# Hybrid mixer: the block inverse and its transpose from vector-engine transpositions, the last doubling in three interleaved steps, the values' factor as a scale on the scalar engine

## The chip, the cores and the metric

The kernel runs on one core of a Trainium2 chip. The metric is the device time of one execution in microseconds; the median of several executions stands for a kernel. Five engines work side by side: the matrix engine (PE), the vector engine (DVE), the scalar engine (ACT), GpSimd (POOL) and the sync engine (SP), which issues the DMA transfers. Matrix products land in PSUM banks; DVE and ACT read them out into SBUF.

## What is computed

A two-layer network on 256 tokens of width 1024, in fp32: each layer is a feed-forward block, a mixer and another feed-forward block, each with a residual and a layer norm. The mixer of layer 0 is a hybrid of a gated delta rule and a state-space scan; that of layer 1 is sparse attention. The change lies in the delta rule of the hybrid mixer. Cut to what matters:

```python
def gated_delta_rule(q, k, v, g, beta):
    ...
    decay = decay_matrix(g_cum)
    strict = np.tril(np.ones((c, c), dtype=bool), -1)
    k_beta = k * beta[..., None]
    a_low = jnp.where(strict, jnp.einsum('bhncd,bhnsd->bhncs', k_beta, k) * decay, 0.0)
    rhs = jnp.concatenate([v * beta[..., None], k_beta * jnp.exp(g_cum)[..., None]], axis=-1)
    sol = lax.linalg.triangular_solve(a_low, rhs, left_side=True, lower=True, unit_diagonal=True)
    u, w = sol[..., :dv], sol[..., dv:]
    ...
    def step(state, inp):
        ...
        v_new = u_c - jnp.einsum('bhck,bhkv->bhcv', w_c, state)
        o_c = jnp.einsum('bhck,bhkv->bhcv', q_c, state) + jnp.einsum('bhcs,bhsv->bhcv', a_c, v_new)
        ...
```

There are 8 heads. k is normalised to length 1 first. The reference solves a unit lower triangular system per head and chunk; the kernel forms the inverse of the triangular matrix and multiplies with it.

## The kernel before

The kernel doesn't issue its instructions in the order in which they are written. All operations of the program are first collected by `Plan.add`; `Plan.order` (line 317) then simulates the engines with a price for every operation, and puts out one order for each engine; `Plan.emit` (line 497) issues it. That is why every instruction of the profile carries line 512: what tells groups apart are the tile names. At each step the planner takes, over all engines, the operation that can start earliest, and among those of one engine the one with the lower priority number (its place in the written program):

```python
key = (st if st > f + 1e-9 else f, p)
```

Here `f` is the time at which the engine is free, `st` the earliest start and `p` the priority. On PE, products that use only a quarter of the array (at most 64 rows of contraction) are told apart from the others; once such a product has run, every other product has 1,000,000 (`turn_pen`) added to `p`, so that quarters that are ready go on first. Operations written with `self.copy` may be put on ACT or DVE, whichever is free earlier. The planner also hands out the buffers: SBUF tiles of tag `m4` (36), weight landing tiles `raw` (4), PSUM banks `ps` (2), `mp` (2) and `acc` (4).

`hybrid` (line 1066) is woven from five strands by `weave` (line 745): `delta` (the delta rule), `space` (the convolutions of the values and of the scan's inputs), `gate`, `space2` (the scan) and `out_a` (half of the output projection). Dense projections go through the `ps` banks: each weight tile arrives in `raw`, is split into `whi` (ACT or DVE) and `wlo` (DVE), and three products of fp32r parts make one fp32 product. The projection's result is copied out of `ps` by ACT (tile `cv`), three DVE steps make the convolution, and ACT applies the nonlinearity.

In `delta` the 256 tokens are two blocks (b = 0, 1) of 128, each with two chunks of 64. Per block and head `AT` holds the transposed triangular matrix. Its inverse is built from 16x16 blocks:

- The 16x16 diagonal blocks are gathered by 32-partition copies into `Z` (in tile `sw`), transposed by one DVE transposition of 32x32 blocks into `Zt`, and inverted by 15 elimination steps on DVE (tile `W` in `sw`), for all blocks at once. After step 8 (`ZERO_AT`) a gate (`late`) releases DMA fills that write zeros into `Ys` and `Tt`.
- Two masked copies of `W` go to `Z`, a DVE transposition makes `Zt`, and narrow copies put the blocks onto the diagonal of `Y` (one tile per block of tokens). PE transposes each `Y` by heads (16 transpositions through `acc` banks), and copies of 64 partitions put the result into `X`. `Y` and `X` are the inverse in both forms.
- Two doublings (`lev` 4 and 5) join 16 to 32 and 32 to 64. Each does 32 products of `AT` with half of `X` into `pT`, a masked copy into `Tt`, then 32 products each into `pY` and `pX` that correct `Y` and `X`. Consecutive products lie in alternating quarters of the array.
- The last doubling joins the two chunks of 64: eight products of `AT` with `X` for each block into `pT[b]` (contraction over rows 0 to 63, result in partitions 64 to 127), a copy into `Tt`, then eight products of `Tt` with `Y` for each block into `pY[b]` (rows 64 to 127, result in partitions 0 to 63), subtracted from `Y`. All of one kind come before the other.

The values: in `space`, after their convolution (`vT`), PE transposes them four heads at a time into an `mp` bank, and one DVE operation for four heads multiplies with `rkinv`, the length of k (one factor for each token and pair of heads), into `vt`. `vt` is what the inverse is multiplied with.

Of fp32 products each shows as two records in the profile, transpositions and fp32r products as one.

Of the kernel before, what the change touches and what calls it, by code (L numbers as in the profile page):

```python
# [12 lines left out]
AF = mybir.ActivationFunctionType  # L13
OP = mybir.AluOpType
# [4 lines left out]
P = 128  # L19
# [31 lines left out]
def H3(t, h):  # L51
    return t.rearrange("p (h t) -> p h t", h=h)
# [483 lines left out]
class K:  # L536
# [529 lines left out]
    def hybrid(self, x, then):  # L1066
        self.arena = None
        nc, i = self.nc, self.i
        V = nc.vector
# [12 lines left out]
        pt = self.bank("mp")  # L1082
# [26 lines left out]
        pt = self.bank("mp")  # L1109
# [42 lines left out]
        def gdn_conv(dests, banks=("ps", "ps")):  # L1152
            for n in range(0, len(dests), 2):
                w = self.unit_cols(w_in, dests[n][0] * P, 256)
                for e in range(2):
                    c, dst = dests[n + e]
                    ps = self.bank(banks[e])[:, :T]
                    yield from self.proj_steps(x, w[e], ps)
                    self.conv_tile(ps, cw, 0, 16, c, None, dst)
# [6 lines left out]
        for n, src in enumerate((kT, qT)):  # L1166
            sq = H3(self.m4(1024, "sq"), 4)
            nc.scalar.activation(sq, src, AF.Square)
            for h in range(4):
                o, c = n * 4 + h, h % 2  # L1170
                nc.tensor.matmul(pn[c * 32:(c + 1) * 32], one_of[:, 31 - o:63 - o], sq[:, h, :],
                                 start=n == 0 and h < 2, stop=n == 1 and h > 1, tile_position=(0, c * 32))
# [13 lines left out]
        rkinv = self.sm([P, 2, 4], "rkinv")  # L1186
# [13 lines left out]
        def delta():  # L1200

            for b in range(2):
# [11 lines left out]
                AT = H3(self.m4(1024, f"AT{b}"), 8)  # L1214
# [9 lines left out]
            QS = [slice(32 * Q, 32 * Q + 32) for Q in range(4)]  # L1224
            sw = [self.m4(1024, f"sw{n}") for n in range(2)]
            z5 = lambda t: t.rearrange("p (r a b h) -> p r a b h", r=16, a=2, b=2)
            a4 = lambda t: t.rearrange("p (r a c) -> p r a c", r=16, a=2)
            Z, Zt = sw[0][:, :512], sw[0][:, 512:]
# [20 lines left out]
            for e in range(2):  # L1249
                V.tensor_scalar(a4(Z)[:, :, e, :], W, hm[:, e:e + 1], None, OP.mult)  # L1250
            V.transpose(Zt, Z)

            X, Tt = (H3(self.m4(1024, n, "D"), 16) for n in ("X", "T"))
            Ys = [H3(self.m4(1024, f"Y{b}", "D"), 8) for b in range(2)]
            with late:
                for t in Ys + [Tt]:
                    self.zero(t)
            CP = [slice(0, 64), slice(64, 128)]
            for b, Y in enumerate(Ys):
                for Q in range(4):  # L1260
                    self.copy(Y[QS[Q], :, QS[Q]].rearrange("p h (a r) -> p h a r", a=2),
                              z5(Zt)[QS[Q], :, :, b, :].rearrange("p r a h -> p h a r"))
                for q in range(2):
                    yield
                    pt = self.bank("acc")
                    for h in range(4):
                        nc.tensor.transpose(pt[:, h * P:(h + 1) * P], Y[:, q * 4 + h, :], self.ident)
                    for cp in CP:
                        self.copy(X[cp, b * 8 + q * 4:b * 8 + q * 4 + 4, :], H3(pt, 4)[cp, :, cp])
                blk[b]['Y'] = Y  # L1270
            AT = [d['AT'] for d in blk]
            heads = [(b, h, cp, b * 8 + h) for b in range(2) for h in range(8) for cp in CP]
            for lev in (4, 5):
                n = 1 << lev
# [5 lines left out]
                pT = self.bank("acc")  # L1280
# [4 lines left out]
                pX, pY = self.bank("acc"), self.bank("acc")  # L1285
                for b, h, cp, k in heads:
                    nc.tensor.matmul(pY[cp, k * 32:(k + 1) * 32], Tt[cp, k, :], half(Ys[b][cp, :, cp], 1)[:, h],
                                     start=True, stop=True)
# [7 lines left out]
                if lev < 5:  # L1296
                    self.zero(Tt)

            yield
            pT = [self.bank("acc") for b in range(2)]  # L1300
            for b in range(2):
                for h in range(8):
                    nc.tensor.matmul(pT[b][64:128, h * 64:(h + 1) * 64], AT[b][0:64, h, 64:128], X[0:64, b * 8 + h, :],
                                     start=True, stop=True)
                self.copy(Tt[64:128, b * 8:b * 8 + 8], H3(pT[b], 8)[64:128])
            yield
            pY = [self.bank("acc") for b in range(2)]
            for b, Y in enumerate(Ys):
                for h in range(8):
                    nc.tensor.matmul(pY[b][0:64, h * 64:(h + 1) * 64], Tt[64:128, b * 8 + h, :], Y[64:128, h, 64:128],  # L1310
                                     start=True, stop=True)
                V.tensor_tensor(Y[0:64, :, 64:128], Y[0:64, :, 64:128], H3(pY[b], 8)[0:64], OP.subtract)

            kd = H3(self.m4(1024, "kd"), 8)
            pt = self.bank("acc")
# [9 lines left out]
            for b, d in enumerate(blk):  # L1325
# [3 lines left out]
                vt, Y, attnT = vts[b], d['Y'], d['attnT']  # L1329
# [29 lines left out]
            for b, d in enumerate(blk):  # L1359
                tb = slice(b * P, (b + 1) * P)  # L1360
                attnT, vn = d['attnT'], d['vn']
                o = H3(self.m4(1024, f"o{b}"), 8)
# [37 lines left out]
        def space():  # L1400
            nonlocal bcT, xT, snw
            vT = [H3(self.m4(1024, f"vT{n}"), 4) for n in range(2)]
            yield from gdn_conv([(8 + n, vT[n // 4][:, n % 4, :]) for n in range(8)])

            for b, d in enumerate(blk):
                tb = slice(b * P, (b + 1) * P)
                vt = H3(self.m4(1024, f"vt{b}"), 8)
                for q in range(2):
                    yield
                    pt = self.bank("mp")  # L1410
                    for h in range(4):
                        nc.tensor.transpose(pt[:, h * P:(h + 1) * P], vT[q][:, h, tb], self.ident)
                    V.tensor_tensor(vt[:, q * 4:q * 4 + 4, :].rearrange("p (h r) t -> p h r t", r=2),
                                    pt.rearrange("p (h r t) -> p h r t", h=2, r=2),
                                    rkinv[:, b, q * 2:q * 2 + 2, None, None].to_broadcast([P, 2, 2, P]), OP.mult)
                vts[b] = vt

            snw = self.m4(1024, "snw", "S")
            with self.late():
                nc.sync.dma_start(snw, i['ssd_norm_w'].partition_broadcast(P).rearrange("p a d -> p (a d)"))  # L1420
            bcT = H3(self.m4(1024, "bcT", "S"), 4)
            xT = [H3(self.m4(1024, f"xT{n}", "S"), 4) for n in range(2)]
            dests = [(8 + n, bcT[:, n, :]) for n in (0, 2, 1, 3)] + [(n, xT[n // 4][:, n % 4, :]) for n in range(8)]
            for n in range(0, 12, 2):
                ws = [self.unit_cols(w_in, 4112 + dests[n][0] * P, 256)] if n > 2 else []
                for e in range(2):
                    c, dst = dests[n + e]
                    w = ws[0][e] if ws else self.unit_cols(w_in, 4112 + c * P, P)[0]
                    ps = self.bank("ps")[:, :T]
                    yield from self.proj_steps(x, w, ps)  # L1430
                    self.conv_tile(ps, cw, 64, 12, c, cw[:, 112 + c:113 + c], dst)
                if n in (6, 10):
                    over.append(n)
# [72 lines left out]
        acc = []  # L1506

        def out_a():
# [3 lines left out]
            for s in range(4):  # L1512
                wo = self.unit_rows(w_out, 2 * s, 2, 0, D)
                for e in range(2):
                    for b in range(2):
                        for c in range(2):
                            cs = slice(c * 512, (c + 1) * 512)
                            self.mm3(acc[b][c], self.xb(oT[0], b, 2 * s + e), (wo[e][0][:, cs], wo[e][1][:, cs]),
                                     s + e == 0, False)
                        yield  # L1520
        self.weave(list(zip((delta(), space(), gate(), space2(), out_a()), W_HYB)))
        terms = []
        for s in range(4):
# [497 lines left out]
```

## Time and profile before

| | |
|---|---|
| median of 3 executions | 1125.7 us |
| lowest, highest | 1124.62, 1126.05 us |
| the profiled execution | 1125.37 us |
| its span | 1123.7 us |
| granted clock of PE | 0.998 |
| HBM read | 194.04 MB |

The span runs from the first to the last instruction; the rest of the execution's time lies around it. "Busy" of PE comes from matmul ends that are modelled, so neighbouring records overlap; where an exact cost is wanted, the distance from the start of one group to the start of the next is used. In rows of groups the columns are: engine, operation, tile written <- tiles read, shapes, count, then busy us and mean ns of one, then the idle time of the engine before them and what ended it. In the order of time they are: start us, length us, engine, operation, tiles, shapes, count, and in brackets the idle time before and its releaser. Small tiles share tiles called `arena`.

### The profile page before, as it was taken

The page shows a single profiled execution, that of the slowest core. Times are in us where ns is not written, and L with a number is a line of the kernel's source. Part 1 is how long each engine was busy: PE and PEld are TensorE (multiplying, and loading weights), DVE is VectorE, ACT ScalarE, POOL GpSimd, SP SyncE. Part 2 cuts the span into 40 slices and gives each one's busy share as a digit, 9 for nine tenths or more (in the row PEclk, how much of TensorE's full clock was granted, in tenths as well). Part 3 has the DMA queues.
Part 4 walks back from the last instruction along what each step waited for, and adds up shares of the span by engine and source line. Part 5 has one row for each costly group of instructions (what it writes and reads, how often), then busy time and mean ns, then how long its engine had stood idle before and what let it go on. Part 6 is the DMA issues. An engine that isn't in the chain of part 4 may idle for free.

```text
span 1123.7 us, 16474 instructions
## 1 busy us (share of the span) xinstructions
PE 1109.8 (99%) x6548; PEld 946.3 (84%) x6548; DVE 887.7 (79%) x1491; ACT 514.9 (46%) x916; POOL 60.5 (5%) x110
## 2 busy tenths in 40 slices
PE   9999999999999999999999999999999999999997
PEld 7888888899999888888888888888877768888886
DVE  6977768799979998777767967876879999777755
ACT  6635332277736565533433633432346656443320
POOL 1000000012001310000000000000002100000000
PEclk9999999999999999999999999999999999999999
DMA  9966562642833285755563756555435237755511
GB/s 332 326 227 199 186 213 80 187 132 61 247 130 114 76 263 187 262 188 188 187 216 121 250 200 192 188 190 154 150 95 206 76 120 241 239 188 192 183 38 37
DMA packets 148710, 198.37 MB, mean 177 GB/s; under 512 B 9341, under 2 KB 123418, under 8 KB 148634
## 3 DMA queue, kind: packets, MB, share of 16 engines
q1 hardware_dynamic: 148634, 197.33, 53.7%
q8 instruction: 51, 0.84, 0.3%
q14 instruction: 25, 0.20, 0.1%
HBM read 194.04 MB, written 1.05 MB: 174 GB/s over the span
## 4 chain that ended last, share of the span: by engine, by line
PE 88%; DVE 9%; ACT 1%; issue 1%; DMA 0%; DVEq 0%; POOL 0%; ACTq 0%; POOLq 0%
PE ps L512 50%; PE acc L512 32%; PE mp L512 5%; DVE wlo L512 2%; DVE cv L512 2%; DVE arena L512 1%; DVE sw L512 1%; DVE qs L512 1%; DMA raw<-in_nsa_w_out_dram 0%; DVE whi L512 0%; DVE AT L512 0%; ACT cv L512 0%; ACT L512 0%; DVE h L512 0%; DVE X L512 0%
## 5 line engine op out<-in xcount | busy, mean ns | idle before, releaser
L512 DVE TENSOR_TENSOR wlo<-raw,whi 128x1024 fp32r<-128x1024 f32 (+1 forms) x349 | 416.0, 1214 | 13.4 <-ACT whi L512 10.6
L512 PE MATMUL ps<-x,whi 128*128 128x512 f32 (+2 forms) x1584 | 369.8, 363 | 1.4 <-ACT cv L512 1.0
L512 PEld LDWEIGHTS ps<-x,whi 128*128 128x128 f32 (+1 forms) x1584 | 278.9, 188 | 45.9 <-ACT cv L512 2.3
L512 ACT ACTIVATE whi<-raw 128x1024 fp32r<-128x1024 f32 x263 | 265.0, 1051 | 15.2 <-DMA raw<-in_ffn_w_in_dram 7.4
L512 PE MATMUL acc<-whi,g 128*128 128x512 f32 x704 | 230.3, 391 | 0.0
L512 PE MATMUL ps<-x,wlo 128*128 128x256 f32 x1368 | 222.2, 283 | 0.0
L512 ACT ACTIVATE sg<-ps 128x256 f32<-128x256 f32 x156 | 60.0, 384 | 345.0 <-PE ps L512 345.0
L512 PEld LDWEIGHTS ps<-x,wlo 128*128 128x128 f32 x1368 | 197.6, 190 | 11.6 <-issue 0.4
L512 DVE TENSOR_TENSOR sg<-ps,sg 128x256 f32<-128x256 f32 (+1 forms) x158 | 67.4, 427 | 161.1 <-ACT sg L512 160.5
L512 PEld LDWEIGHTS acc<-whi,g 128*128 128x128 f32 x704 | 132.5, 188 | 26.0
L512 PE MATMUL acc<-wlo,g 128*128 128x512 f32 x352 | 138.1, 392 | 0.0
L512 PE MATMUL ps<-whi,x 128*128 128x512 f32 (+1 forms) x480 | 128.1, 385 | 0.0
L512 PEld LDWEIGHTS ps<-whi,x 128*128 128x128 f32 x480 | 86.1, 188 | 15.7 <-issue 0.9
L512 PEld LDWEIGHTS acc<-wlo,g 128*128 128x128 f32 x352 | 66.4, 189 | 10.9
L512 PE MATMUL acc<-whi,x 128*128 128x512 f32 x224 | 73.5, 403 | 1.6 <-DVE x L512 0.9
L512 PE MATMUL ps<-wlo,x 128*128 128x512 f32 (+1 forms) x240 | 67.0, 380 | 0.0
L512 DVE CAST whi<-raw 128x1024 fp32r<-128x1024 f32 (+1 forms) x86 | 59.1, 687 | 0.5 <-DMA raw<-in_nsa_w_out_dram 0.5
L512 POOL TENSOR_TENSOR lnve<-lnve,mhalf 128x1 f32<-128x1 f32 x12 | 11.5, 957 | 741.7 <-DVE lnve L512 741.7
L512 PEld LDWEIGHTS acc<-whi,x 128*128 128x128 f32 x224 | 41.1, 188 | 11.1 <-DVE x L512 1.7
L512 PEld LDWEIGHTS ps<-wlo,x 128*128 128x128 f32 x240 | 43.3, 188 | 7.8 <-issue 0.5
L512 ACT ACTIVATE sg<-sg 128x256 f32<-128x256 f32 x72 | 30.1, 418 | 34.8 <-DVE sg L512 34.7
L512 PE MATMUL acc<-wlo,x 128*128 128x512 f32 x112 | 43.2, 402 | 0.0
(258 smaller groups left out, 1011.0 us busy)
## 6 DMA issues: line engine op xcount, KB each, us to landing
raw<-in_ffn_w_in_dram SPq DMA_DIRECT2D x72, 1024.0 KB, 5.2
raw<-in_ffn_w_out_dram SPq DMA_DIRECT2D x44, 1024.0 KB, 5.0
raw<-in_hyb_w_in_dram SPq DMA_DIRECT2D x20, 1024.0 KB, 5.2
raw<-in_ffn_w_in_dram SPq DMA_DIRECT2D x32, 512.0 KB, 5.0
raw<-in_hyb_w_out_dram SPq DMA_DIRECT2D x8, 1024.0 KB, 5.2
raw<-in_nsa_w_in_dram SPq DMA_DIRECT2D x5, 1024.0 KB, 5.6
raw<-in_nsa_cmp_w_dram SPq DMA_DIRECT2D x4, 1024.0 KB, 5.9
raw<-in_nsa_w_out_dram SPq DMA_DIRECT2D x4, 1024.0 KB, 6.2
```

What stands on the lines that cost most here:

```text
L512: r = getattr(getattr(nc, eng), fn)(*[res(a) for a in args], **{k: res(a) for k, a in kw.items()})
```

## The change

Three edits in `hybrid`:

1. A second DVE transposition `Zx` of `Z`, read in another order, gives the blocks in the other form. `X` is filled from it by eight copies of 32 partitions, next to the eight of `Y`. The 16 transpositions on PE, their `acc` banks and the eight 64-partition copies are gone. As the new copies write only the diagonal blocks, `X` gets a zero fill by DMA, between those of `Ys` and `Tt`.
2. The last doubling is written in three steps: the first block's eight products into `pT`; then, one by one, the second block's into `pT` and the first block's into `pY`, which lie in opposite quarters; then the second block's into `pY`. Both subtractions come after.
3. The values' factor is applied by ACT, as the scale of a copy out of PSUM: two heads at a time (eight operations of 256 columns) in place of four DVE operations of 512.

```diff
@@ -1249,24 +1249,23 @@
             for e in range(2):
                 V.tensor_scalar(a4(Z)[:, :, e, :], W, hm[:, e:e + 1], None, OP.mult)
             V.transpose(Zt, Z)
+            Zx = sw[1][:, :512]
+            V.transpose(Zx, Z.rearrange("p (r a c) -> p c a r", r=16, a=2))
 
             X, Tt = (H3(self.m4(1024, n, "D"), 16) for n in ("X", "T"))
             Ys = [H3(self.m4(1024, f"Y{b}", "D"), 8) for b in range(2)]
             with late:
-                for t in Ys + [Tt]:
+                for t in Ys + [X, Tt]:
                     self.zero(t)
             CP = [slice(0, 64), slice(64, 128)]
             for b, Y in enumerate(Ys):
                 for Q in range(4):
                     self.copy(Y[QS[Q], :, QS[Q]].rearrange("p h (a r) -> p h a r", a=2),
                               z5(Zt)[QS[Q], :, :, b, :].rearrange("p r a h -> p h a r"))
-                for q in range(2):
-                    yield
-                    pt = self.bank("acc")
-                    for h in range(4):
-                        nc.tensor.transpose(pt[:, h * P:(h + 1) * P], Y[:, q * 4 + h, :], self.ident)
-                    for cp in CP:
-                        self.copy(X[cp, b * 8 + q * 4:b * 8 + q * 4 + 4, :], H3(pt, 4)[cp, :, cp])
+                    o = Q % 2 * 32
+                    self.copy(X[QS[Q], b * 8:b * 8 + 8, o:o + 32].rearrange("p h (a r) -> p h a r", a=2),
+                              z5(Zx)[QS[Q], :, :, b, :].rearrange("p r a h -> p h a r"))
+                yield
                 blk[b]['Y'] = Y
             AT = [d['AT'] for d in blk]
             heads = [(b, h, cp, b * 8 + h) for b in range(2) for h in range(8) for cp in CP]
@@ -1296,19 +1295,29 @@
                 if lev < 5:
                     self.zero(Tt)
 
+            pT = [self.bank("acc") for b in range(2)]
+            pY = [self.bank("acc") for b in range(2)]
+
+            def couple(b, h):
+                nc.tensor.matmul(pT[b][64:128, h * 64:(h + 1) * 64], AT[b][0:64, h, 64:128], X[0:64, b * 8 + h, :],
+                                 start=True, stop=True)
+
+            def back(b, h):
+                nc.tensor.matmul(pY[b][0:64, h * 64:(h + 1) * 64], Tt[64:128, b * 8 + h, :], Ys[b][64:128, h, 64:128],
+                                 start=True, stop=True)
             yield
-            pT = [self.bank("acc") for b in range(2)]
-            for b in range(2):
-                for h in range(8):
-                    nc.tensor.matmul(pT[b][64:128, h * 64:(h + 1) * 64], AT[b][0:64, h, 64:128], X[0:64, b * 8 + h, :],
-                                     start=True, stop=True)
-                self.copy(Tt[64:128, b * 8:b * 8 + 8], H3(pT[b], 8)[64:128])
+            for h in range(8):
+                couple(0, h)
+            self.copy(Tt[64:128, 0:8], H3(pT[0], 8)[64:128])
             yield
-            pY = [self.bank("acc") for b in range(2)]
+            for h in range(8):
+                couple(1, h)
+                back(0, h)
+            self.copy(Tt[64:128, 8:16], H3(pT[1], 8)[64:128])
+            yield
+            for h in range(8):
+                back(1, h)
             for b, Y in enumerate(Ys):
-                for h in range(8):
-                    nc.tensor.matmul(pY[b][0:64, h * 64:(h + 1) * 64], Tt[64:128, b * 8 + h, :], Y[64:128, h, 64:128],
-                                     start=True, stop=True)
                 V.tensor_tensor(Y[0:64, :, 64:128], Y[0:64, :, 64:128], H3(pY[b], 8)[0:64], OP.subtract)
 
             kd = H3(self.m4(1024, "kd"), 8)
@@ -1410,9 +1419,10 @@
                     pt = self.bank("mp")
                     for h in range(4):
                         nc.tensor.transpose(pt[:, h * P:(h + 1) * P], vT[q][:, h, tb], self.ident)
-                    V.tensor_tensor(vt[:, q * 4:q * 4 + 4, :].rearrange("p (h r) t -> p h r t", r=2),
-                                    pt.rearrange("p (h r t) -> p h r t", h=2, r=2),
-                                    rkinv[:, b, q * 2:q * 2 + 2, None, None].to_broadcast([P, 2, 2, P]), OP.mult)
+                    for h in range(2):
+                        n = q * 2 + h
+                        nc.scalar.activation(vt[:, n * 2:n * 2 + 2, :], H3(pt, 4)[:, h * 2:h * 2 + 2, :], AF.Copy,
+                                             scale=rkinv[:, b, n:n + 1])
                 vts[b] = vt
 
             snw = self.m4(1024, "snw", "S")
```

## The prediction

> **What bounds the kernel now.** I read the page first (shares of the engines, the chain that ended last), then the table of windows over the stage that the change touches, then the order of time on the matrix engine (PE) around the edited lines.
>
> ```profile
> span 1123.7 us, 16474 instructions
> PE 1109.8 (99%) x6548; PEld 946.3 (84%) x6548; DVE 887.7 (79%) x1491; ACT 514.9 (46%) x916; POOL 60.5 (5%) x110
> ...
> PE 88%; DVE 9%; ACT 1%; issue 1%; DMA 0%; DVEq 0%; POOL 0%; ACTq 0%; POOLq 0%
> ```
>
> PE is busy for 1109.8 of 1123.7 us; the chain runs over it for 88% of the span. The vector engine's 9% lie mostly in one place, so that place needs its own table (columns: PE, PEld, DVE, ACT, POOL busy, clock, DMA share, GB/s).
>
> ```profile
> 200.00:460.00 260.00, 258.81 (x1993) 229.45 (x1993) 233.67 (x442) 155.87 (x246) 33.53 (x50) 1.00 0.50 161
> ...
> 265.00:275.00 10.00, 8.97 (x66) 8.13 (x65) 9.94 (x24) 8.10 (x15) 0.00 (x0) 1.00 0.20 54
> 275.00:285.00 10.00, 10.00 (x86) 10.00 (x85) 10.00 (x30) 6.88 (x13) 0.00 (x0) 1.00 0.54 158
> 285.00:295.00 10.00, 10.00 (x80) 9.49 (x79) 10.00 (x27) 6.88 (x13) 0.00 (x0) 1.00 1.01 290
> ...
> 300.00:306.00 6.00, 5.93 (x83) 5.40 (x81) 5.35 (x15) 4.91 (x11) 0.00 (x0) 1.00 0.64 224
> ```
>
> Over the 260 us around the mixer PE stands still for 1.19 us, and 1.03 us of that is one gap in 265 to 275. DVE is as full as PE from 265 to 295, and there the chain hops onto it. Still, PE has no second gap there: it always finds projection work. So I take PE's work as the bound: an edit counts by what PE no longer has to issue or to wait for, and DVE's relief counts only where PE stands.
>
> **The change part by part.** First PE's own order around the inverse.
>
> ```profile
> 302.08 0.28 PE L512 MATMUL ps<-x,whi 128*128 128x256 f32 x1
> 302.20 1.91 PE L512 MATMUL acc<-ident,Y 128*128 128x128 f32 x16
> 304.04 2.63 PE L512 MATMUL acc<-X,AT 64*64 64x32 f32 x64
> 306.61 0.39 PE L512 MATMUL ps<-x,whi 128*128 128x256 f32 x1
> ...
> 314.76 2.06 PE L512 MATMUL acc<-X,AT 64*64 64x32 f32 x64
> 316.75 0.39 PE L512 MATMUL ps<-x,whi 128*128 128x256 f32 x1
> ```
>
> (a) *The 16 transpositions leave PE.* They hold it from 302.20 to 304.04: 1.84 us, 115 ns each. Nothing else covers them, as PE never pauses there, so the whole 1.84 us is gain.
>
> (b) *The wait behind them.* The first group of level 4 holds PE from 304.04 to 306.61, 2.57 us; the same 64 records at level 5 take 316.75 - 314.76 = 1.99 us. So 0.58 us is waiting for the second block's X, whose last copy comes late. Is X earlier afterwards? Rows:
>
> ```profile
> L512 DVE STREAM_TRANSPOSE sw<-sw 128x512 f32<-128x512 f32 x2 | 1.4, 704 | 0.0
> ...
> L512 DVE COPY Y<-sw 32x256 f32<-32x256 f32 x6 | 2.3, 389 | 0.1
> ...
> L512 DVE COPY X<-acc 64x256 f32<-64x256 f32 x4 | 1.6, 419 | 0.5 <-ACT X L512 0.5
> ...
> L512 DVE TENSOR_SCALAR sw<-sw,arena 128x256 f32<-128x256 f32 x3 | 1.0, 348 | 0.0
> ```
> ```profile
> L512 ACT ACTIVATE X<-acc 64x256 f32<-64x256 f32 x4 | 1.4, 375 | 1.0 <-DVE X L512 0.7 <-issue 0.3
> ...
> L512 ACT ACTIVATE Y<-sw 32x256 f32<-32x256 f32 x2 | 1.3, 667 | 0.0
> ```
> ```profile
> 299.20 0.70 DVE L512 STREAM_TRANSPOSE sw<-sw 128x512 f32<-128x512 f32 x1
> ...
> 300.19 2.42 DVE L512 COPY Y<-sw 32x256 f32<-32x256 f32 x6
> ...
> 305.60 0.38 ACT L512 ACTIVATE X<-acc 64x256 f32<-64x256 f32 x1 [0.71 <-DVE X L512]
> ```
>
> Now X is whole at 305.98. The new second transposition reads with a stride, which no row shows for this operation; its bounds are 0.704 us (the contiguous one) and 0.704 + 2 x 0.04 = 0.78 us (a strided copy of 256 elements costs 389 ns, a contiguous pass over 256 costs 348). I take 0.70, nearer to the row of the same operation. The 16 copies now cost 6 x 0.389 + 4 x 0.419 + 2 x 0.667 + 4 x 0.375 = 6.8 us of both engines. Sixteen narrow ones, eleven on DVE and five on ACT as their speeds have it, cost 7.6 us: 0.8 more, 0.4 for each engine. The pauses between the copies (0.5 us on DVE, 1.0 on ACT, 0.75 in the mean) fall away with PE's part. So X is whole at 305.98 + 0.70 + 0.4 - 0.75 = 306.3, no earlier by itself, and the wait could stay. What can bring it forward is DVE's relief in (d). Bounds: 0.58 us gained, or 0.3 us lost. I take 0.45 gained, since the relief is larger than what X loses here.
>
> (c) *Last doubling.*
>
> ```profile
> 324.79 2.08 PE L512 MATMUL acc<-X,AT 64*64 64x64 f32 x32
> 326.79 0.39 PE L512 MATMUL ps<-x,whi 128*128 128x256 f32 x1
> ...
> 327.45 2.08 PE L512 MATMUL acc<-Y,T 64*64 64x64 f32 x32
> ```
> ```profile
> 325.96 0.69 DVE L512 COPY T<-acc 64x512 f32<-64x512 f32 x1 [1.35 <-PE acc L512]
> ```
>
> 32 records (16 products) of 64 columns take 2.00 us, 62.5 ns each; level 5's 32-column ones, which alternate quarters, take 31 ns. By column that is the same, so these rows do not say that alternating quarters is faster. A row with alternating column strips does:
>
> ```profile
> 243.22 1.06 PE L512 MATMUL mp<-sq,arena 128*32 128x256 f32 x8
> 244.21 0.39 PE L512 MATMUL ps<-x,whi 128*128 128x256 f32 x1
> ```
> ```profile
> 346.59 0.87 PE acc L512 x4
> ```
>
> Eight 256-column records in 0.99 us are 124 ns each against 218 ns for full-array ones. So the middle 32 records would cost between 31 and 62.5 ns: a gain of 0 to 1.0 us *if they alternate*. I expect that they don't, so that this part doesn't do what it says. The planner sorts by earliest start first, then priority (line 434). The second block's eight `couple` products are ready together with the first's, and while PE is in quarter mode everything else is put back by 1,000,000 (line 430). The first `back` needs the copy of T, which ends at 325.96 + 0.69 = 326.65; in the same trace the second couple group ends at 326.79. So PE will issue couple 0, couple 1, then back 0, back 1, exactly as now. Gain taken: 0.
>
> The Trainium skill speaks of this in "TensorEngine Tiling (Array Packing)", Key Properties: different tiles of the array work independently, in parallel. The strip rows agree, the 32-column rows show no sign of it. By that rule an alternating order would give the full 1.0 us; the order decides whether it can.
>
> (d) *The values' factor.*
>
> ```profile
> L512 DVE TENSOR_TENSOR vt<-mp,arena 128x512 f32<-128x512 f32 x4 | 2.7, 684 | 0.0
> ```
> ```profile
> L512 ACT ACTIVATE cv<-cv,arena 128x256 f32<-128x256 f32 x28 | 15.3, 546 | 0.6
> L512 ACT ACTIVATE cv<-ps 128x256 f32<-128x256 f32 x24 | 9.1, 378 | 9.5 <-PE ps L512 9.5
> ...
> L512 ACT ACTIVATE x<-mp 128x512 fp32r<-128x512 f32 x7 | 4.1, 597 | 15.1 <-PE mp L512 12.3 <-PE ps L512 2.8
> ...
> L512 ACT ACTIVATE x<-mp,arena 128x512 fp32r<-128x512 f32 x3 | 2.1, 690 | 2.2 <-PE mp L512 2.2
> ```
>
> DVE loses 4 x 0.684 = 2.74 us inside the two full windows, less 0.70 for the second transposition. ACT gains eight scaled reads of PSUM: bounds 378 ns (unscaled) and 546 ns (scaled, from SBUF); the factor adds 690 - 597 = 93 ns, so 0.47 each, 3.8 us. ACT is busy for 6.88 of 10 us there and waits 9.5 us for PE before its PSUM copies, so it has room. Queued behind these on ACT are the copies that free the two projection banks for PE, and the halves of weights. On PE the sum is 0; without that room it is R3. On DVE the elimination, whose steps each have another instruction put between, loses four such instructions and can end up to 2.7 us sooner; weight halves may take their places.
>
> The Trainium skill speaks against this part: "ScalarE: Activation LUTs", Rules for kernel authors, gives multiplication to VectorE rather than ScalarE. The rows agree on the cost, and by it the part loses 3.8 - 2.7 = 1.1 us wherever ACT is what PE waits for; R3 is that case.
>
> (e) *One more zero fill* on SP's queue, 512 KB ahead of T's fill and three weight loads.
>
> ```profile
> 289.94 3.75 SPq L512 DMA_DIRECT2D T<-zeros  x1
> 293.79 13.72 SPq L512 DMA_DIRECT2D raw<-in_hyb_w_in_dram  x3
> ```
> ```profile
> L512 SPq DMA_DIRECT2D T<-zeros x1: 3750/3750/3750, 289.9 to 289.9; - x1
> ...
> DMA to landing us min/median/max: 9.3/9.3/9.3
> ```
>
> T's fill lands 9.3 us after its issue, at 299.2; X's takes that slot, in time for its first copy, which the second transposition holds back until about 300.6. T's then lands at the rate of the queue, 0.52 MB at 290 GB/s, 1.8 us later, at 301, and is needed only behind the first level 4 group, which ends at 306.61. The three loads land 1.8 us later; PE's cover is the weights already split. Taken at 0; 1.5 us if that cover is gone.
>
> **Sum:** -1.84 - 0.45 + 0 + 0 + 0 = -2.3 us. The profiled execution took 1125.37 us (its span and 1.67 us around it), 0.3 us under the median of 1125.7. So 1123.1 for a run like it and 1123.4 for the median.
>
> **The rivals.** (R1) *Quarters do alternate*: if the planner held back the second couple group, another 1.0 us: 1122.4. Against it stands line 434; for it, only the emitted order. (R2) *The gain is waited away*: PE reaches level 4 sooner, X does not, and the 0.58 us wait grows by up to 1.8 us; 1125.7 - 1.84 + 1.8 = 1125.7, on average about 1125. For it: the 306.3 for X in (b), and a plan redrawn everywhere in a stage with only 1.19 us of standing time, which can hardly fall. (R3) *Slower*: the pairs of scaled reads stand before the copies that free the projection banks. The place shows itself already:
>
> ```profile
> 273.13 0.50 PE L512 MATMUL ps<-x,whi 128*128 128x256 f32 x2 [1.03 <-ACT cv L512]
> ```
>
> PE stood 1.03 us for such a copy. Each pair costs 2 x 0.47 = 0.94 us; it decides once ACT has no slack before that copy. If all four pairs hit: -1.84 + 4 x 0.94 = +1.9, with X's wait grown by 0.3 as in (b) +2.2: 1127.9. Against: ACT mostly waits for PE there. (R4) *DVE is the true bound from 220 to 302*, as the chain's 9% on DVE would have it: its net relief of 2.04 us counts too: 1123.4 - 2.0 = 1121.4. Against: PE at 10.00 of 10.
>
> **How the numbers follow.** A change of under 0.2%, 2.25 us, is not to be told from none here. My forecast has 0.45, R1 0.08, R2 0.25, R3 0.12, R4 0.10. The forecast's own spread runs from 1122.6 to 1124.3, about its middle; the bound for faster is 1123.45, so I give 0.27 of its 0.45 to faster and 0.18 to same. Faster: 0.27 + 0.08 + 0.10 = 0.45. Same: 0.18 + 0.25 + 0.02 (R3 with few pairs) = 0.45. Slower: 0.10. The range goes down to R4's 1121.4 and up to 1126.8, between R2 and R3, leaving about a tenth on each side.
>
> **What would show it.** No `acc<-ident,Y` records; between the dense work the first `acc<-X,AT` group near 2.0 us if (b) holds, longer if R2. Two unbroken runs `acc<-X,AT` and `acc<-Y,T` of 32 records each for (c); a mixed run of 32 in about 1 us would be R1. Scaled `vt<-mp` on ACT near 470 ns; gaps of PE before `ps` ended by ACT would be R3. The stage over 200 to 460 shorter by about 2.3 us with standing time still near 1 us. The forecast is wrong if that standing time rises above 3 us, or if PE's count falls and the span doesn't.

## The result, and the profile after

The changed kernel takes 1127.63 us (median of 12 executions, 1126.53 to 1129.2) against 1125.31 us for the kernel before (12 executions): a ratio of 1.0021, 95% interval 1.0014 to 1.0028. It is 2.3 us slower where 2.3 us faster was forecast. The profiled execution took 1127.84 us with a span of 1126.1.

PE has the 16 instructions less that were to leave it (6548 before), and the span of 1126.1 us doesn't follow (engines' line of the page after):

```profile
PE 1109.3 (99%) x6532; PEld 944.6 (84%) x6532; DVE 888.8 (79%) x1487; ACT 517.9 (46%) x925; POOL 61.5 (5%) x110
```

The windows of the mixer after (PE, PEld, DVE, ACT, POOL busy, clock, DMA share, GB/s) say where:

```profile
200.00:460.00 260.00, 256.65 (x1962) 226.23 (x1962) 232.86 (x434) 157.54 (x252) 34.81 (x50) 1.00 0.50 160
265.00:275.00 10.00, 8.96 (x66) 8.14 (x65) 9.94 (x24) 8.10 (x15) 0.00 (x0) 1.00 0.20 54
...
332.00:340.00 8.00, 7.75 (x59) 7.13 (x58) 6.10 (x11) 4.84 (x9) 0.00 (x0) 1.00 0.21 85
...
380.00:400.00 20.00, 18.45 (x96) 14.34 (x95) 18.55 (x32) 11.57 (x19) 7.93 (x24) 1.00 0.40 146
```

PE's standing time over the stage rose from 1.19 to 3.35 us. The old gap in 265 to 275 is the same (1.04 for 1.03). The new time stands mostly in 380 to 400, 60 us behind the code that was edited. The timeline there, PE before, then after:

```profile
381.13 0.39 PE L512 MATMUL acc<-wlo,x 128*128 128x512 f32 x1
381.36 0.39 PE L512 MATMUL acc<-whi,x 128*128 128x512 f32 x1
381.59 0.60 PE L512 MATMUL mp<-ident,xT 128*128 128x128 f32 x4
```

```profile
375.38 0.60 PE L512 MATMUL mp<-ident,y 128*128 128x128 f32 x4
...
381.30 0.39 PE L512 MATMUL acc<-wlo,x 128*128 128x512 f32 x1
383.09 0.66 PE L512 MATMUL mp<-ident,xT 128*128 128x128 f32 x4 [1.40 <-DVE x L512]
```

The same stretch on DVE, after:

```profile
379.69 2.74 DVE L512 SCALAR_TENSOR_TENSOR o<-o,arena,zg 128x128 f32<-128x128 f32 x6
382.36 0.68 DVE L512 TENSOR_TENSOR x<-mp,x 128x512 fp32r<-128x512 f32 x1
```

and on DVE before:

```profile
380.40 1.28 DVE L512 TENSOR_TENSOR x<-mp,x 128x512 fp32r<-128x512 f32 x2
...
383.93 2.78 DVE L512 SCALAR_TENSOR_TENSOR o<-o,arena,zg 128x128 f32<-128x128 f32 x8
```

Both `mp` banks hold transposed halves of `y`, which only the splits `x<-mp,x` set free. Before, DVE did the two splits first and then the eight steps that scale block 1's output `o`. After, six of the eight come first, and PE, which needs an `mp` bank for `mp<-ident,xT`, waits 1.40 us; it starts 383.09 - 381.30 = 1.79 us after a product that otherwise takes 0.23 (the step from 381.13 to 381.36 before), so the place costs 1.56. What the six steps wait for is the reciprocal root on GpSimd, which comes 3 us sooner, as the delta rule runs ahead (POOL; before, then after):

```profile
379.44 2.56 POOL L512 TENSOR_TENSOR arena<-arena,mhalf 128x8 f32<-128x8 f32 x1 [8.66 <-DVE arena L512]
```
```profile
376.49 2.56 POOL L512 TENSOR_TENSOR arena<-arena,mhalf 128x8 f32<-128x8 f32 x1 [3.46 <-DVE arena L512]
```

None of these instructions was edited: the planner drew the whole stage anew. The edited places themselves, PE after:

```profile
297.66 0.30 PE L512 MATMUL acc<-X,AT 64*64 64x32 f32 x2
298.22 1.45 PE L512 MATMUL acc<-X,AT 64*64 64x32 f32 x32
301.79 1.11 PE L512 MATMUL acc<-X,AT 64*64 64x32 f32 x30
...
314.33 2.06 PE L512 MATMUL acc<-Y,T 64*64 64x32 f32 x64 [0.22 <-DVE T L512]
...
320.31 2.08 PE L512 MATMUL acc<-X,AT 64*64 64x64 f32 x32
...
322.98 2.08 PE L512 MATMUL acc<-Y,T 64*64 64x64 f32 x32
```

No `acc<-ident,Y`; level 4 starts at 297.66 and no longer at 304.04, in three pieces with dense work between them; the last doubling is two unbroken runs, as before.

### The profile page after: what moved, and what is told of

Its sections match the earlier page's. It is cut to its first block, busy times and chain, and to the rows that moved or that the text cites. A ratio compares the mean times of both kernels' runs of the same rounds, so it can differ in the third digit from the quotient of the medians.

```text
span 1126.1 us, 16452 instructions
## 1 busy us (share of the span) xinstructions
PE 1109.3 (99%) x6532; PEld 944.6 (84%) x6532; DVE 888.8 (79%) x1487; ACT 517.9 (46%) x925; POOL 61.5 (5%) x110
## 3 DMA queue, kind: packets, MB, share of 16 engines
HBM read 194.04 MB, written 1.05 MB: 173 GB/s over the span
## 4 chain that ended last, share of the span: by engine, by line
PE 84%; DVE 10%; ACT 2%; issue 2%; DMA 1%; POOL 1%; SPq 0%; DVEq 0%; ACTq 0%; POOLq 0%
PE ps L512 50%; PE acc L512 30%; PE mp L512 4%; DVE wlo L512 2%; DVE cv L512 2%; DVE arena L512 1%; DVE qs L512 1%; DVE o L512 1%; DMA h<-in_x_dram 0%; DMA T<-zeros 0%; POOL arena L512 0%; DMA raw<-in_nsa_w_out_dram 0%; DVE whi L512 0%; DVE AT L512 0%; ACT L512 0%
```

## The experiments

All but the changed kernel itself were timed in five rounds beside the kernel before (median 1125.89, 1125.80 and 1126.02 us in the three sessions, four kernels in each, in the order of their texts: e1, e3, f, g2; f5, fg, e1 with the splits first, xf; b1, b2, h4, p). The kernel before thus moves by 0.7 us from session to session (1125.31 beside the changed kernel), so each ratio is against the one timed beside it. "Standing" is 260 us less PE's busy time in the window 200 to 460.

| run | what it is | median us | ratio, 95% interval | standing us |
|---|---|---|---|---|
| (after) | all three parts | 1127.63 | 1.0021 (1.0014 to 1.0028) | 3.35 |
| e1_transposes | part 1 alone | 1129.44 | 1.0032 (1.0021 to 1.0043) | 4.34 |
| e3_act_scale | part 3 alone | 1126.76 | 1.0005 (0.9996 to 1.0013) | 1.38 |
| g2_alternate | before, quarters made to alternate | 1125.24 | 0.9995 (0.9986 to 1.0004) | 1.26 |
| f_order_at_380 | after, splits first | 1125.44 | 1.0005 (0.9992 to 1.0019) | 1.54 |
| f5_splits_first | after, splits first | 1125.35 | 1.0000 (0.9991 to 1.0009) | 1.46 |
| fg_splits_first_alternate | f5 with alternation | 1125.13 | 0.9996 (0.9988 to 1.0005) | 1.44 |
| e1_splits_first | part 1, splits first | 1127.27 | 1.0017 (1.0005 to 1.0029) | 2.79 |
| xf_fill_only | before, one fill more | 1129.65 | 1.0033 (1.0020 to 1.0045) | 4.27 |
| b1_one_level4_group | after, one group, splits first | 1125.96 | 1.0000 (0.9991 to 1.0008) | 2.81 |
| b2_one_group_alternate | b1 with alternation | 1125.32 | 0.9998 (0.9990 to 1.0007) | 2.54 |
| h4_group_alone | after, one group | 1128.53 | 1.0023 (1.0014 to 1.0033) | 4.32 |
| p_pow_price | after, other price of the root | 1128.11 | 1.0018 (1.0010 to 1.0027) | 3.86 |

Part 2 alone has no run: with it the planner puts out the same instruction streams on every engine as without it.

**The parts alone.** e1 has the second transposition, X's copies and X's fill; e3 has this:

```diff
-                    V.tensor_tensor(vt[:, q * 4:q * 4 + 4, :]...
+                        nc.scalar.activation(vt[:, n * 2:n * 2 + 2, :], ..., AF.Copy, scale=rkinv[:, b, n:n + 1])
```

> Before plus the first edit alone (X from the second vector-engine transposition, zero fill of X, no transpositions on PE). Theory A (the 1.84 us leave PE, but the delta rule runs ahead and, at about 380 us, its last scaling steps `o<-o,arena,zg` stand on DVE ahead of the two `x<-mp,x` that free both mp banks, so that PE waits 1.4 us there): PE gap of 1 to 1.5 us near 381, total within 1 us of before (1124.5 to 1126). Theory B (the loss comes from the third edit, scaled copies on ACT): no new gap, 1.8 to 2.3 us faster, 1123.0 to 1123.5. Theory C (the new copies or the zero fill delay X): gap at the first level 4 group, 0 to 1 us slower.

> Before plus the third edit alone (the values' factor on ACT). Theory A: DVE has both `x<-mp,x` before the scaling steps here, so no gap near 381; PE's work is unchanged: within 1 us of before. Theory B: slower by 2 to 4 us (ACT's 3.7 us of new work in front of the copies that free the projection banks). `vt<-mp,arena` 463 ns each as in the changed kernel.

Part 1 alone is slower than the whole change. Theory A had the gap right and the time wrong: 1129.44 us lies 3.4 us above its 1126. DVE in e1:

```profile
380.51 2.74 DVE L512 SCALAR_TENSOR_TENSOR o<-o,arena,zg 128x128 f32<-128x128 f32 x6
```

and PE in e1:

```profile
306.37 1.11 PE L512 MATMUL acc<-X,AT 64*64 64x32 f32 x30 [0.63 <-DVE X L512]
...
383.90 0.66 PE L512 MATMUL mp<-ident,xT 128*128 128x128 f32 x4 [1.47 <-DVE x L512]
```

The same six steps ahead of the splits, the same gap, and X late at level 4, the gap that theory C looked for. Part 3 alone has neither gap, and its time cannot be told from no change: the scaled copies on ACT do not hold PE up, and with them level 4 starts 4 us sooner (PE in e3):

```profile
300.04 2.01 PE L512 MATMUL acc<-X,AT 64*64 64x32 f32 x50
```

**The order at 380 put back.** The changed kernel with nothing but a planner's price altered; f has 4500 ns, f5 has 5000:

```diff
-            return 830.0 + 130.0 * N
+            return 4500.0 if op.idx == self.slow else 830.0 + 130.0 * N
...
                 nc.gpsimd.tensor_tensor(so[:, 3, :], so[:, 2, :], self.mhalf.to_broadcast([P, 8]), OP.pow)
+                self.plan.slow = len(self.plan.ops) - 1
```

> The changed kernel, in which the planner prices one POOL power at 4500 ns, so that DVE issues both `x<-mp,x` ahead of the second block's `o<-o,arena,zg` steps; all else is the same up to there. Theory A: the gap of 1.40 us near 381 goes, 1126.0 to 1126.6 against 1127.6 for the changed kernel. Theories B and C: the gap only moves, 1127.3 to 1128.

> The changed kernel, its instructions the same; only block 1's reciprocal root on GpSimd is handed to the planner at 5000 ns, so that the two splits x<-mp of the transposed second half come ahead of all eight scaling steps of block 1, as in the kernel before (in f_order_at_380 three steps stood between the second split and the other five). Theory A (the order at 380 is what cost the changed kernel about 1.5 us, the rest of the gain went into small waits elsewhere): no gap of PE over 0.3 us between 379 and 385, and 1125 to 1126 us. Theory R (each redrawn plan has its own waits of 1 to 3 us, and no single place decides): the gap at 380 is gone and another of 0.5 us or more stands elsewhere after 355; 1126 to 1128 us. Theory G (PE's 1.84 us are collected whenever nothing waits): 1123.5 to 1124.3 us.

DVE in f5, and PE in f5:

```profile
379.99 1.29 DVE L513 TENSOR_TENSOR x<-mp,x 128x512 fp32r<-128x512 f32 x2
...
383.09 2.93 DVE L513 SCALAR_TENSOR_TENSOR o<-o,arena,zg 128x128 f32<-128x128 f32 x8
```
```profile
332.61 0.33 PE L513 MATMUL mp<-ident,xT 128*128 128x128 f32 x1 [0.26 <-ACT xT L513]
...
380.98 0.60 PE L513 MATMUL mp<-ident,xT 128*128 128x128 f32 x4
```

The gap is gone, with the root as early as in the changed kernel (375.94), so that DVE's order alone decides. With the gap go 2.2 to 2.3 us of the changed kernel's 1127.63, though not one instruction was added or left out; f came out 0.6 us below theory A's range. Up to 376 us the orders of PE and DVE are the same in f5 and in the changed kernel. There (`mp<-ident,y`, 374.83 against 375.38) the profiled f5 is 0.55 us ahead, and at the next block's first transposition it is 3.10 ahead (428.10 against 431.20), so about 2.5 us lie between. So the order at 380, with what follows from it, is the whole of the loss against the kernel before. It is not all of the loss against the forecast: 1125.35 is 0.45 us under the kernel before timed beside it, inside the interval, and not 1.84.

**Part 1 with the splits first** (f's price in e1).

> The transpositions' part alone (e1_transposes), with the same price for block 1's reciprocal root (4500 ns), so that the splits come ahead of the scaling steps. Theory A: the gap of 1.47 us at 382 is gone, and the time falls from 1129.4 by 1.3 to 1.6 us, to 1127.8 to 1128.2; level 4 still waits for X about 0.7 us at 304 to 306, the vector engine still having the values' scaled copies ahead of X's copies. Theory R: the gap is gone and the time moves by less than 0.8 us.

It fell by 2.2 us, more than theory A said; theory R falls. In what is left above the kernel before are waits for X (0.66 us), S (0.49) and xT (0.32). PE in this run, and a window of it:

```profile
305.62 1.11 PE L513 MATMUL acc<-X,AT 64*64 64x32 f32 x30 [0.66 <-DVE X L513]
```
```profile
307.00:310.60 3.60, 3.60 (x22) 3.38 (x22) 3.60 (x8) 2.60 (x5) 0.00 (x0) 0.53 0.37 133
```

The window shows something that the waits don't: the clock granted to PE is 0.53 in these 3.6 us, which begin 1.4 us after the wait for X ended, and 1.00 in the 9 us before and after. Six of the eleven executions of this kernel have a mean granted clock below 0.998, against one of the 27 of the kernel before beside it; the other five have a median of 1126.34 us. So a part of the 1.5 us above the kernel before is the clock and not the plan.

**One fill more, and nothing else.**

```diff
-                for t in Ys + [Tt]:
+                for t in Ys + [X, Tt]:
```

> The kernel before with one thing added: X is filled with zeros by a transfer, too, though its copies overwrite all of it. No instruction of PE, DVE, ACT or POOL is added or removed; only the planner sees one more transfer, and draws its plan anew from there. Theory A (the transfer itself costs): X's copies come at 303 to 306, long after a fill issued at 286 to 290 has landed, so 1125.7 within 0.5 us. Theory R (a redrawn plan scatters by a microsecond or more whatever was changed): the time differs from 1125.7 by 0.8 us or more, most likely upwards, with PE's count and busy time as before and its standing time larger at places without X.

3.85 us slower, the slowest of all, without one instruction of the four computing engines added or removed (four copies moved from ACT to DVE). DVE and PE in this run:

```profile
380.22 1.96 DVE L512 SCALAR_TENSOR_TENSOR o<-o,arena,zg 128x128 f32<-128x128 f32 x3
...
382.70 1.27 DVE L512 TENSOR_TENSOR x<-mp,x 128x512 fp32r<-128x512 f32 x2
```
```profile
383.43 0.66 PE L512 MATMUL mp<-ident,xT 128*128 128x128 f32 x4 [1.61 <-DVE x L512]
```

The kernel before falls into the same hole when its plan is redrawn for a transfer that it doesn't need: theory A falls, theory R holds. Most of it stands from 381 to 388 (this gap, and 0.56 and 0.70 us behind it), over 80 us after the fill; level 4 itself starts at 304.76, close to the 304.04 of before. Not every redrawn plan does so: e3 and g2 stand for 1.38 and 1.26 us, without a gap at 380.

**Quarters made to alternate.** In the kernel before with part 2 (g2), and in f5 (fg), the second block's couples wait for the copy of the first block's:

```diff
+            held = _Gate(self.plan, len(self.plan.ops) - 1)
             yield
             for h in range(8):
-                couple(1, h)
+                with held:
+                    couple(1, h)
                 back(0, h)
```

> Before plus the second edit, with the second block's couple products held back until the first block's copy of T, so that 16 products alternate between opposite quarters. If opposite quarters run side by side: the 32 alternating records take 1.0 us instead of 2.0, PE's work falls by up to 1.0 us, less one more turn between quarter and full products (0.1 to 0.25 us); 0.5 to 1 us faster. If not: 2.0 us, and 0 to 0.5 us slower.

> f5_splits_first with the last doubling's couples of block 1 held back to the copy of block 0's, so that the quarters alternate. By g2_alternate the 32 alternating records take 1.07 us where two unbroken groups of 16 took 2.0; the term of 0.65 us measured there should come off here again if dense work fills PE behind it: 0.5 to 0.9 us under f5_splits_first, 1124.3 to 1125.2 us. Theory R: the plan is redrawn once more and the difference to f5_splits_first is anywhere from -0.9 to +1 us, with gaps at places that have nothing to do with the last doubling.

PE in g2 (the pairs between go on in the same step):

```profile
325.86 1.11 PE L512 MATMUL acc<-X,AT 64*64 64x64 f32 x16
...
328.15 0.22 PE L512 MATMUL acc<-X,AT 64*64 64x64 f32 x1
328.16 0.22 PE L512 MATMUL acc<-Y,T 64*64 64x64 f32 x1
...
328.97 0.22 PE L512 MATMUL acc<-X,AT 64*64 64x64 f32 x1
328.98 0.22 PE L512 MATMUL acc<-Y,T 64*64 64x64 f32 x1
...
330.12 1.14 PE L512 MATMUL acc<-Y,T 64*64 64x64 f32 x16
```

From 328.15 to 328.97 are 14 pairs, 58.6 ns each: two opposite quarters run in the time of one (62.5 ns for a single record in an unbroken run). In the kernel's time this is 0.65 us in g2's medians and 0.22 in fg's against f5's, both inside the intervals, so no run shows it in the time; the expectation of 0.5 to 0.9 for fg was missed.

**Level 4 in one group again.** The first products of level 4 wait for X's last copy; h4 has this alone, b1 adds a price of 5500 ns for the root, b2 the alternation as well:

```diff
+            copied = _Gate(self.plan, len(self.plan.ops) - 1)
             AT = [d['AT'] for d in blk]
...
+                with copied if lev < 5 else _Gate(self.plan, None):
```

> The changed kernel with level 4's first products in one group and nothing done about the order at 380 (six scaling steps stay ahead of the splits). Theory A: the two turns come off and the gap near 381 stays at 1.0 to 1.7 us; 1127.0 to 1127.4 us against the changed kernel's 1127.63. If the groups and not the order were what cost: 1126 us or less.

> The changed kernel's instructions; level 4's first products wait for the last copy into X, so that they are one group of 128 again and not three of 8, 32 and 88, and block 1's reciprocal root is priced 5500 ns, so that the two splits stand ahead of the eight scaling steps as before. Theory A (order at 380 plus small costs that can be named: two more turns between the whole array and its quarters, some 0.2 us each from the starts of records, and one wait for xT of 0.26 us at 332): two turns less, no gap over 0.3 us, 0.3 to 0.5 us under f5_splits_first's 1125.35, so 1124.8 to 1125.1 us. Theory R (each redrawn plan has waits of its own): a new gap of 0.5 us or more somewhere and 1125.5 us or more.

> b1_one_level4_group with the couples of block 1 held back to the copy of block 0's, so that the last doubling's quarters alternate: the three parts of the edit as the change describes them, with the splits first. Theory A: the alternation takes off another 0.3 to 0.9 us (g2_alternate: 0.65; f5 to fg: 0.22 in the median), 1124.0 to 1124.8 us, 1.0 to 1.8 us under the kernel before. Theory R: a new gap, and 1125.3 us or more.

By their medians all three missed theory A's times on the slow side. Turns did come off, and a wait came in their place, here in b1 on PE, and on DVE what it waits for:

```profile
310.90 2.05 PE L513 MATMUL acc<-X,AT 64*64 64x32 f32 x64 [0.75 <-DVE X L513]
```
```profile
308.43 1.71 DVE L513 TENSOR_TENSOR Y<-Y,acc 64x256 f32<-64x256 f32 x4
310.16 0.69 DVE L513 TENSOR_TENSOR X<-X,acc 128x512 f32<-128x512 f32 x1
```

Level 5 waits for X's correction, which stands behind four of Y's on DVE. In h4 the gap at 380 is 1.47 us with six scaling steps in front, as expected. So a turn saved at one place was a wait at the next, as theory R has it.

Not all of the misses is that wait. A window of b1:

```profile
313.00:317.00 4.00, 4.00 (x22) 4.00 (x23) 1.72 (x3) 0.88 (x3) 0.00 (x0) 0.57 0.58 179
```

Behind the wait the granted clock falls again: 16 projection products step 213 ns apart from 313.1 to 316.5, and 119 ns apart after it, an estimate of 1.5 us lost. The profiled b2 has the same from 314.0 to 317.4 (granted clock 0.50). h4 has the same wait (0.80 us) and a clock of 1.00 behind it, so what brings the fall on isn't shown. The executions with a mean granted clock of 0.998 or more have medians of 1125.86 us (b1), 1125.05 (b2) and 1127.51 (h4): still above theory A's ranges (by 0.8, 0.3 and 0.1 us), and b2's is below theory R's 1125.3. How much the wait cost and how much the clock isn't separated.

**A truer price for the root.**

```diff
-            return 830.0 + 130.0 * N
+            return 830.0 + 220.0 * N
```

> The changed kernel's instructions; all reciprocal roots on GpSimd are handed to the planner at 830 + 220 ns per column, which gives 2590 ns for 8 columns where the traces show 2.56 (the kernel's 830 + 130 gives 1870). Theory P (the planner draws a bad order at 380 because it takes the root for 0.7 us shorter than it is): with the right price its order has no gap there, 1125 to 1126 us. Theory A': the order at 380 depends on which of two ready groups of the vector engine has the higher priority, not on that price; the plan puts all eight scaling steps ahead of the splits and the gap near 381 is 1.5 to 2.5 us, 1127.5 to 1129 us.

DVE and PE in this run:

```profile
376.68 3.64 DVE L512 SCALAR_TENSOR_TENSOR o<-o,arena,zg 128x128 f32<-128x128 f32 x8
...
383.65 1.27 DVE L512 TENSOR_TENSOR x<-mp,x 128x512 fp32r<-128x512 f32 x2
```
```profile
384.38 0.66 PE L512 MATMUL mp<-ident,xT 128*128 128x128 f32 x4 [1.18 <-DVE x L512]
```

All eight steps come ahead, with three weight halves between them and the splits, and PE waits 1.18 us (1.5 to 2.5 expected; the time is inside the range of theory A'). Theory P falls: a true price does not cure the order. As it changes the price of every such root, PE's order differs from the changed kernel's from 243 us on, so the run says no more than that.

## Why the prediction was wrong

The step that failed stands at its head: "PE ... always finds projection work. So I take PE's work as the bound: an edit counts by what PE no longer has to issue or to wait for." That held for the plan of before, whose 1.19 us of standing time belong to that one order. An edit that makes the planner draw another order brings standing time of that order's own: in the changed kernel PE stood 1.40 us at 381 for an `mp` bank, and with the order there put back 2.2 to 2.3 us went. Eight kernels with the very same computing instructions (after, f, f5, fg, b1, b2, h4, p) lie between 1125.13 and 1128.53 us, a spread of 3.4 us (3.2 if each is taken against the kernel before beside it), larger than every term of the sum. All five plans with the gap of 1.2 to 1.6 us at 380 (after, e1, xf, h4, p) are at 1127.6 or more; with the splits first the changed kernel's instructions are at 1125.1 to 1126.0, and part 1's at 1127.3.

- (a) Half right: the 16 transpositions left PE, but "the whole 1.84 us is gain" failed. The times show no gain clear of noise, even with the order at 380 put back (f5: a ratio of 1.0000, 0.9991 to 1.0009); in f5's trace the work is 0.76 us ahead, as told below.
- (b) The direction was wrong for X. It was forecast at 306.3, and ACT's last copy into it ends at 299.33 + 0.64 = 299.97. Its copies cost what was estimated, the strided transposition more (1.11 us for 0.70, above the bound of 0.78), but all of it starts sooner: DVE's first transposition at 294.50 and not at 299.20. e3 shows part 3 alone bringing level 4 forward by 4 us; the prediction named this relief, and gave it only the worth of the 0.58 us wait. Being early was worth little: level 4 now went in three pieces. A visit to the quarters costs about 0.2 us (the turns into and out of them take 209 and 149 ns from start to start in f5, where a 256-column product by itself takes 120 and a quarter record 36), so 0.4 us for two more. In f5 the three pieces hold PE for 0.23, 1.39 and 1.05 us, 2.67 in all, against 2.57 for the one group of before, and the turns into two more pieces add 0.3: 0.4 us lost where 0.45 gained were forecast.
- (c) Right: no alternation, no gain, by line 434. Its price if it alternates came out at 29 ns a record, just under the lower bound of the 31 to 62.5 given. (The 218 ns for full-array records, to which the strip's 124 were compared, come from the chain, where the last record's length counts too; from start to start these four take 347.11 - 346.43 = 0.68 us, 170 ns each. No term rests on it.) The Trainium skill, "TensorEngine Tiling (Array Packing)", Key Properties, has different tiles of the array work independently and in parallel; g2's trace agrees.
- (d) Right on the engines: ACT's scaled reads took 0.46 us each (0.47 estimated) and no gap before `ps` grew, so R3 did not happen. The Trainium skill, "ScalarE: Activation LUTs", Rules for kernel authors, would have kept this multiplication on VectorE. The rows agree on the cost (two reads of 0.46 us on ACT for one of 0.68 on DVE), and the time doesn't show it: e3's 1126.76 us cannot be told from the kernel before.

```profile
L512 ACT ACTIVATE vt<-mp,arena 128x256 f32<-128x256 f32 x8 | 3.2, 464 | 0.0
```

- (e) X's fill hid, as said. T's second fill did not quite in the profiled execution (DVE waits 0.52 us for it, and PE 0.22 for DVE, at 313 to 314; f5, with the same order there, shows neither wait), and what the fill does to the plan was not thought of:

```profile
313.59 0.69 DVE L512 TENSOR_TENSOR T<-acc,arena 128x512 f32<-128x512 f32 x1 [0.52 <-DMA T<-zeros]
```

Of the rivals R2 came nearest: it named "a plan redrawn everywhere in a stage with only 1.19 us of standing time, which can hardly fall", but looked for the wait at X and priced it at 1.8 us at most, at a time still no slower than before. R3 priced a slower outcome, by the wrong mechanism. The prediction's own sign of failure, standing time above 3 us, came true.

The kernel with the order put back (f5) still misses (a)'s 1.84 us. In the traces its work reaches the next block's first transposition 0.76 us sooner (PE before, then f5):

```profile
428.86 0.60 PE L512 MATMUL mp<-ident,h 128*128 128x128 f32 x4
```
```profile
428.10 0.60 PE L513 MATMUL mp<-ident,h 128*128 128x128 f32 x4
```

Of the other 1.08 us, 0.4 are level 4 in three pieces and about 0.4 the wait for xT at 332 with the restart behind it; 0.3 have no place that stands out. What stays open is why the planner's rule sends the scaling steps first in so many plans: a true price of the root was tried and does not cure it, others were not. What brings on the lower granted clock behind the waits for X in three of the traces is open as well. No version beat the kernel before by more than the interval; fg and b2 come lowest, 0.7 us under it in the median.

## What to carry to other kernels

Where a planner redraws the order, a saving is worth what the new order leaves of it, so look for the next places where two strands meet at a buffer (here two PSUM banks against a chain of scaling steps), and ask which strand the edit makes early. A redraw control, an edit that changes the plan and no work, tells how much of a small difference belongs to the edit at all: here it moved the time by 3.85 us, and the whole change by 2.3. Look at the granted clock of the stage too, before a difference of 1 us is put down to a wait. Once such a place is found, pin the order there, and measure the edit with the order held.

## What the hardware showed besides

The DVE transposition of 128x512 with a strided read took longer than the contiguous one: the two in the changed kernel take 1.74 us together (0.906 in the mean, so 1.11 for the strided one), where the contiguous one takes 0.70.

```profile
294.50 1.74 DVE L512 STREAM_TRANSPOSE sw<-sw 128x512 f32<-128x512 f32 x2
```

The reciprocal root of 128x8 on GpSimd takes two durations in one trace, 2.56 us at 379.44 and this (before):

```profile
365.24 1.65 POOL L512 TENSOR_TENSOR arena<-arena,mhalf 128x8 f32<-128x8 f32 x1 [7.98 <-DVE arena L512]
```

In e3 and g2 both roots take 1.65 us. What sets the one or the other wasn't tried.

In three traces (e1 with the splits first, b1, b2) the clock granted to PE fell to about half for 3.4 us, shortly after a wait of 0.66 to 0.80 us before a group of quarter products; the other traces with such a wait there (e1, h4, p) and the 1.40 us gap at 380 show no such fall.
